# State-space mixer: decay, convolution and gate work moved from GpSimd to VectorE and ScalarE

## Chip, cores and metric

The kernel runs on one core of a Trainium2 chip. The metric is device time in microseconds of one execution; the numbers of record are the median over several executions. Engines are named as in the profile: PE is TensorE, DVE is VectorE, ACT is ScalarE, POOL is GpSimd, SP is the engine whose queue issues most DMAs.

## The reference, cut to what matters

The program is a stack of twelve units (attention, state space, feed-forward, mixture of experts). The change touches one of them, a bidirectional state-space mixer over 256 positions, 32 heads of 64, 8 groups of B and C with state size 128:

```python
def ssd_mixer(h, w_in, conv_w, conv_b, dt_bias, a_log, d_skip, norm_g, w_out):
    z, xbc, dt_raw = split(h @ w_in)
    xbc = silu(centred_depthwise_conv(xbc, conv_w, conv_b))      # 5 taps
    xs, b_f, c_f, b_b, c_b = split(xbc)
    dt = softplus(dt_raw + dt_bias)
    a = -exp(a_log)
    y_fwd = ssd_scan(xs, dt[:, :, 0], a[0], b_f, c_f)
    y_bwd = flip(ssd_scan(flip(xs), flip(dt[:, :, 1]), a[1], flip(b_b), flip(c_b)))
    y = y_fwd + y_bwd + xs * d_skip
    return rmsnorm_2(y * silu(z), norm_g) @ w_out

def ssd_scan(x, dt, a, b_mat, c_mat):                            # chunks of 128
    cum = cumsum(dt * a)
    seg = cum[t] - cum[s]
    scores = (C[t] . B[s]) * exp(where(s <= t, seg, -inf)) * dt[s]
    y = scores @ x          # and, across the chunk border, the same with the decay over it
```

## The kernel before, in words

All weights are f32 in HBM and reach SBUF as tiles of 1 MB (`wraw`), by DMAs on SP's queue in program order; three raw tiles are held. Every tile is split on chip into a rounded part and a rest: ACT writes `whi` (L211), DVE subtracts it and writes `wlo` (L212), in two halves of 128x1024 each; three split tiles are held. A projection of 256 output columns is 48 matmuls (L269): for each of 8 k-blocks and 2 column blocks three products, of `whi` and `wlo` with the two parts `hh` and `hl` of the activations. Results stand in three PSUM banks `pj`; four banks `acc` serve the scan.

The mixer (`ssd`, L1920) runs over 8 groups g. For each group it projects four tiles, in the order x, f (B and C forward), b (B and C backward), z:

- `conv` (L1929) evacuates x, f or b from PSUM with the norm's row factor (`cz`, L1931, DVE), starts the convolution on ACT (L1936) and adds four more taps to each of two halves: by `stt` (L287, DVE, in place in `cvx`, `cvf`, `cvb`), but for the second half of x by a product `cvt` (L1942) and a sum (L1943) on POOL. ACT applies silu (L1947).
- `ssd_decay` (L1896) makes the decays of a group for both directions r: SP loads the group's rows of the cumulative sums, broadcast to 128 partitions, into `crow` (two DMAs of 512 KB, one buffer). POOL subtracts the per-partition part (L1911), adds the causal mask, 0 or -1e30 (L1912), for the two diagonal blocks, and adds the offset of the block between the chunks (L1915). ACT takes exp in place (L1917). The tile `E` is 128x4x3x128 (4 heads, 3 blocks), in three buffers.
- `scan` (L1956) transposes x on PE, copies it to `xd` (ACT, L1966), multiplies B with C on PE into a PSUM bank (6 matmuls of 128 columns) and multiplies `E` by that bank on DVE (L1975, 128x1536, ahead in priority by 100).
- `scan_out` (L1978) multiplies `E` with `xd` on PE (16 matmuls a group, `acc<-E,xd`), adds the skip term on DVE (two `stt`), multiplies by the gate `sz` on POOL (L1990), splits the result into `yh` (ACT, L1994) and `yl` (DVE), and sums its squares (ACT L410, POOL L419 and L420).

In the program text the loop over g projects x, f, then runs `scan(g-1)`, projects b and z, then runs `scan_out(g-1)` and `ssd_decay(g)`. After the loop come `scan(7)`, `scan_out(7)` and the output projection: 8 tiles of 48 matmuls (`acc<-yh,whi` and the like, 384 in all). A scheduler orders each engine's instructions at build time, from program order and the priorities in the text; at run time each engine, and SP's queue, takes its list strictly in order and waits on semaphores.

Of the kernel before, what the change touches and what calls it, by code (L numbers as in the profile page):

```python
# [27 lines left out]
NEG = -1e30  # L28

# [217 lines left out]
class Kernel:  # L247
# [1587 lines left out]
    def ssd_consts(self, pool):  # L1835
        nc = self.nc
        S = self.S = {}
        S["mask"] = [pool.tile([128, 128], F32, name=f"smask{i}") for i in range(2)]
        for m, op in zip(S["mask"], (OP.is_lt, OP.is_gt)):
            nc.vector.tensor_scalar(m, self.jp, 0.0, NEG, op0=op, op1=OP.mult)  # L1840
        go = S["go"] = pool.tile([64, T], F32, name="sgo")
        nc.gpsimd.memset(go, 1.0)
        nc.gpsimd.memset(go.rearrange("p (c i) -> p c i", i=128)[:, :, 0:1], 0.0)
        na = S["na"] = pool.tile([64, 32], F32, name="sna")[:, 0:1]
        nc.scalar.activation(na, self.v["a_log"][:64, :], AF.Exp)
        nc.vector.tensor_scalar(na, na, -1.0, None, op0=OP.mult)
        S["cz"] = {}
        for n, k in (("x", 2), ("f", 1), ("b", 1)):
            for i in range(k):
                z = S["cz"][n, i] = pool.tile([128, 2, T + 4], F32, name=f"cz{n}{i}")  # L1850
                nc.gpsimd.memset(z[:, :, 0:2], 0.0)
                nc.gpsimd.memset(z[:, :, T + 2:T + 4], 0.0)

    def ssd_dt(self, pool, b, r):
# [31 lines left out]
        for o, c, l in ((0, 0, 127), (32, 1, 128)):  # L1886
            rs, cs = slice(o, o + 32), slice(c * 128, (c + 1) * 128)
            self.stt(off[rs], dt[rs, cs], cum[rs, l:l + 1], cum[rs, cs], OP.add, OP.subtract)
        v.tensor_sub(p, cum, dt)
        b = self.bank("ms")  # L1890
        for i, src in enumerate((p[:, 0:128], p[:, 128:256], off)):
# [4 lines left out]
    def ssd_decay(self, pool, g):  # L1896


        nc, S = self.nc, self.S
        cr = pool.tile([128, 2, 4, T], F32, name="crow", bufs=1)  # L1900
        src = S["dram"].rearrange("(r h) t -> r h t", r=2)[:, 4 * g:4 * g + 4, :]
        for r in range(2):
            nc.sync.dma_start(cr[:, r], src[r][None].to_broadcast([128, 4, T]))
        out = []
        for r in range(2):
            E = pool.tile([128, 4, 3, 128], F32, name="E", bufs=3)
            hs = slice(4 * g, 4 * g + 4)
            for c in range(2):
                d = E[:, :, 2 * c, :]
                cc = S["tok"][:, c, r, hs][:, :, None].to_broadcast([128, 4, 128])  # L1910
                nc.gpsimd.tensor_sub(d, cr[:, r, :, c * 128:(c + 1) * 128], cc)  # L1911
                nc.gpsimd.tensor_add(d, d, S["mask"][r][:, None, :].to_broadcast([128, 4, 128]))  # L1912
            oc = S["tok"][:, 2, r, hs][:, :, None].to_broadcast([128, 4, 128])
            t = slice(128, 256) if r == 0 else slice(0, 128)
            nc.gpsimd.tensor_add(E[:, :, 1, :], cr[:, r, :, t], oc)  # L1915
            out.append(E)
            nc.scalar.activation(E, E, AF.Exp)  # L1917
        return out

    def ssd(self, pool, tail):  # L1920
# [8 lines left out]
        def conv(n, g, b):  # L1929
# [7 lines left out]
            for k in range(1, 5):  # L1937
                for j in range(2):
                    w = cw[:, 48 * k + tl[j]:48 * k + tl[j] + 1]
                    if n == "x" and j:  # L1940
                        t = pool.tile([128, T], F32, name="cvt", bufs=1)
                        nc.gpsimd.tensor_mul(t, z[:, j, k:k + T], w.to_broadcast([128, T]))  # L1942
                        nc.gpsimd.tensor_add(c[:, j], c[:, j], t)  # L1943
                    else:
                        self.stt(c[:, j, :], z[:, j, k:k + T], w, c[:, j, :], OP.mult, OP.add)
# [10 lines left out]
        def scan(g, tag="acc"):  # L1956
# [10 lines left out]
            for r, bc in enumerate((fb, bb)):  # L1967
# [4 lines left out]
                cb = b[:, None, 0:384].to_broadcast([128, 4, 384])  # L1972
                e = E[r].rearrange("p h i t -> p h (i t)")
                with self.tc.high_priority(offset=100):
                    v.tensor_mul(e, e, cb)  # L1975
            D_["s", g] = E, xs, xd, sz

        def scan_out(g, tag="acc"):  # L1978
# [11 lines left out]
            nc.gpsimd.tensor_mul(sz, sz, xs)  # L1990
# [19 lines left out]
        for g in range(8):  # L2010
            for n in "xfb":
                if (n, g) != ("x", 0):
                    self.proj([("ssd", n, g)], lambda i, b: conv(n, g, b))
                if n == "f" and g:
                    scan(g - 1)
            self.proj([("ssd", "z", g)], lambda i, b: gate(g, b))
            if g:
                scan_out(g - 1)
            D_["E", g] = self.ssd_decay(pool, g)
# [496 lines left out]
```

## Time and profile before

| what | value |
|---|---|
| median of 3 runs | 2814.09 us (2808.49 to 2814.82) |
| the profiled execution | 2806.44 us |
| its span in the trace | 2804.6 us |
| the mixer's part of the span | from about 1677 us to 2024 us |
| DVE, PE, ACT, POOL busy, whole span | 78%, 93%, 56%, 20% |

The span is the time between the first and the last instruction in the trace; the profiled execution's own time is 1.8 us longer. Busy shares are unions over an engine's instructions. "Idle before" in a row is the time in which the engine stood still just ahead of those instructions, with what ended it. A row's busy time divided by its count is what one instruction takes of its engine when they follow each other; the mean ns is longer, since the start of one overlaps the end of the one before.

### The profile page before, as it was taken

The numbers are of one execution on the slowest core, as the hardware profiler recorded it, in microseconds if no ns is written. First come the engines' busy times: TensorE is split into PE (matmuls) and PEld (weight loads), VectorE is DVE, ScalarE is ACT, GpSimd is POOL, SyncE is SP. The second block draws the span as 40 slices with busy tenths as digits, with TensorE's granted clock in tenths as the row PEclk, the third lists the DMA queues.
The fourth block names the chain that finished last, engine by engine and source line by source line (L and its number), as shares of the span: only waits on it lengthen the run. The fifth ranks groups of instructions, "written<-read, shape, count | busy, mean of one in ns | idle before, by whom it ended". The sixth has DMA issues, their size and how long they took to land. (4 is left out here: it accounts for less than half of the span.)

```text
span 2804.6 us, 50551 instructions
## 1 busy us (share of the span) xinstructions
PE 2622.2 (93%) x20739; PEld 2446.0 (87%) x20739; DVE 2178.5 (78%) x3100; ACT 1582.7 (56%) x2222; POOL 564.0 (20%) x490
## 2 busy tenths in 40 slices
PE   8999968989999999999998998887899999989999
PEld 6789967789999999999778997777799999979998
DVE  6989986869998999988876568999665675665666
ACT  5343336657777777777663445766444454465444
POOL 2413982310000000000000005776110010240000
PEclk9999988999999999999998999999999999999999
DMA  7476764256999999999763554434445555552553
GB/s 276 167 270 248 279 210 150 91 214 258 349 338 355 339 353 365 342 325 372 250 213 140 197 178 152 151 139 147 151 166 196 186 175 193 195 188 72 182 194 121
DMA packets 109203, 623.07 MB, mean 222 GB/s; under 512 B 10049, under 2 KB 10065, under 8 KB 56353
## 3 DMA queue, kind: packets, MB, share of 16 engines
q1 hardware_dynamic: 107664, 612.05, 61.2%
q0 software_dynamic: 1296, 7.68, 0.7%
q8 instruction: 165, 2.70, 0.4%
q14 instruction: 78, 0.63, 0.1%
HBM read 616.49 MB, written 3.21 MB: 221 GB/s over the span
## 5 line engine op out<-in xcount | busy, mean ns | idle before, releaser
L212 DVE TENSOR_TENSOR wlo<-wraw,whi 128x1024 fp32r<-128x1024 f32 (+1 forms) x1046 | 1284.3, 1265 | 250.1 <-ACT whi L211 247.3
L211 ACT ACTIVATE whi<-wraw 128x1024 fp32r<-128x1024 f32 (+1 forms) x1046 | 1046.5, 1050 | 668.6 <-issue 353.8
L269 PE MATMUL pj<-hh,whi 128*128 128x256 f32 (+1 forms) x2672 | 757.8, 284 | 54.0 <-DVE czb L1931 38.5
L269 PE MATMUL pj<-hh,wlo 128*128 128x256 f32 (+1 forms) x2672 | 754.3, 282 | 4.1 <-DVE wlo L212 4.0
L269 PE MATMUL pj<-hl,whi 128*128 128x256 f32 (+1 forms) x2672 | 754.2, 282 | 1.2 <-DVE hl L287 1.2
L269 PEld LDWEIGHTS pj<-hh,whi 128*128 128x128 f32 (+1 forms) x2672 | 514.9, 193 | 58.9 <-issue 29.3
L269 PEld LDWEIGHTS pj<-hh,wlo 128*128 128x128 f32 (+1 forms) x2672 | 514.4, 193 | 7.9 <-DVE wlo L212 6.8
L269 PEld LDWEIGHTS pj<-hl,whi 128*128 128x128 f32 (+1 forms) x2672 | 514.8, 193 | 3.0 <-DVE hl L287 2.3
L269 PE MATMUL pj<-whi,hg 128*128 128x256 f32 x2112 | 382.2, 279 | 0.0
L269 PEld LDWEIGHTS pj<-whi,hg 128*128 128x128 f32 x2112 | 325.6, 188 | 11.2 <-issue 8.7
L269 PE MATMUL pj<-wlo,hg 128*128 128x256 f32 x1056 | 294.0, 278 | 0.0
L269 PE MATMUL acc<-mh,whi 128*128 128x256 f32 x880 | 245.5, 279 | 13.9 <-ACT whi L211 13.9
L269 PE MATMUL acc<-mh,wlo 128*128 128x256 f32 x880 | 245.8, 279 | 7.0 <-DVE wlo L212 7.0
L269 PE MATMUL acc<-ml,whi 128*128 128x256 f32 x880 | 245.7, 279 | 1.6 <-DVE ml L284 1.6
L269 PEld LDWEIGHTS pj<-wlo,hg 128*128 128x128 f32 x1056 | 198.6, 188 | 3.7 <-issue 2.1
L269 PEld LDWEIGHTS acc<-mh,whi 128*128 128x128 f32 x880 | 167.2, 190 | 14.1 <-ACT whi L211 14.1
L441 POOL TENSOR_TENSOR rc<-var,mhalf 128x2 f32<-128x2 f32 x2 | 1.4, 705 | 878.4 <-DVE var L1803 877.1
L417 POOL TENSOR_TENSOR ss<-sq 128x256 f32<-128x256 f32 x11 | 11.9, 1083 | 825.1 <-ACT sq L410 592.2
L269 PEld LDWEIGHTS acc<-mh,wlo 128*128 128x128 f32 x880 | 167.1, 190 | 8.1 <-DVE wlo L212 8.1
L269 PEld LDWEIGHTS acc<-ml,whi 128*128 128x128 f32 x880 | 167.1, 190 | 2.2 <-DVE ml L284 2.2
L269 PE MATMUL acc<-whi,mml 128*128 128x512 f32 x352 | 139.1, 399 | 0.7 <-DVE mml L284 0.7
L269 PE MATMUL acc<-wlo,mmh 128*128 128x512 f32 x352 | 139.6, 397 | 0.0
(721 smaller groups left out, 4424.6 us busy)
## 6 DMA issues: line engine op xcount, KB each, us to landing
wraw<-in_o_exp_down_dram SPq DMA_DIRECT2D x88, 1024.0 KB, 5.8
wraw<-in_ffn_w_gu_dram SPq DMA_DIRECT2D x88, 1024.0 KB, 5.0
wraw<-in_o_exp_gate_dram SPq DMA_DIRECT2D x87, 1024.0 KB, 5.9
wraw<-in_o_exp_up_dram SPq DMA_DIRECT2D x87, 1024.0 KB, 6.0
wraw<-in_ffn_w_down_dram SPq DMA_DIRECT2D x44, 1024.0 KB, 5.1
wraw<-in_ssd_cols_dram SPq DMA_DIRECT2D x32, 1024.0 KB, 4.9
wraw<-in_e_mod_ffn_w_t_dram SPq DMA_DIRECT2D x12, 1024.0 KB, 5.0
wraw<-in_o_mod_mix_w_t_dram SPq DMA_DIRECT2D x12, 1024.0 KB, 5.0
```

Source lines behind the costliest of these rows:

```text
L211: nc.scalar.activation(hi[:, cs], t[:, cs], AF.Copy)
L212: nc.vector.tensor_sub(lo[:, cs], t[:, cs], f32(hi[:, cs]))
L269: self.nc.tensor.matmul(out, lhsT, rhs, start=start, stop=stop, skip_group_check=True)
L417: nc.gpsimd.tensor_add(ss[0], sq[:, 0, :], sq[:, 1, :])
L441: nc.gpsimd.tensor_tensor(r, v, self.mhalf.to_broadcast([128, n]), op=OP.pow)
```

## The change

The masks become factors 0 and 1. Both blocks' per-partition parts and the block between the chunks now have one sign, so that one subtraction serves all three blocks. SP loads the broadcast rows straight into `E` (four DMAs a group: two of 4x256 and two of 4x128 elements per partition, in pieces of 1024 and 512 bytes; 1.5 MB in place of 1 MB), now with four buffers for `E` and none for `crow`. DVE subtracts (one 128x1536 instruction a direction) and limits the diagonal blocks to 88.722 (one `min` over 1024 elements). ACT takes exp as before. The mask is multiplied onto the product of B and C on its way out of PSUM (`scb`: DVE two blocks, ACT copies the third), and the product with `E` reads `scb` from SBUF. The second half of x's convolution and the gate product go to DVE. `ssd_decay(g)` is called right after x's projection of group g. POOL keeps only the sums of squares.

```diff
--- before.py
+++ after.py
@@ -26,6 +26,8 @@
 MID = 3
 EPS = 1e-6
 NEG = -1e30
+
+LOGMAX = 88.722
 
 SPLIT_ORDER = {"s": -30, "f1_0": -100, "e": -200, "f2_0": 50}
 
@@ -1836,8 +1838,8 @@
         nc = self.nc
         S = self.S = {}
         S["mask"] = [pool.tile([128, 128], F32, name=f"smask{i}") for i in range(2)]
-        for m, op in zip(S["mask"], (OP.is_lt, OP.is_gt)):
-            nc.vector.tensor_scalar(m, self.jp, 0.0, NEG, op0=op, op1=OP.mult)
+        for m, op in zip(S["mask"], (OP.is_ge, OP.is_le)):
+            nc.vector.tensor_scalar(m, self.jp, 0.0, None, op0=op)
         go = S["go"] = pool.tile([64, T], F32, name="sgo")
         nc.gpsimd.memset(go, 1.0)
         nc.gpsimd.memset(go.rearrange("p (c i) -> p c i", i=128)[:, :, 0:1], 0.0)
@@ -1885,10 +1887,10 @@
         off = s2[:, 0:128]
         for o, c, l in ((0, 0, 127), (32, 1, 128)):
             rs, cs = slice(o, o + 32), slice(c * 128, (c + 1) * 128)
-            self.stt(off[rs], dt[rs, cs], cum[rs, l:l + 1], cum[rs, cs], OP.add, OP.subtract)
+            self.stt(off[rs], cum[rs, cs], cum[rs, l:l + 1], dt[rs, cs], OP.subtract, OP.subtract)
         v.tensor_sub(p, cum, dt)
         b = self.bank("ms")
-        for i, src in enumerate((p[:, 0:128], p[:, 128:256], off)):
+        for i, src in enumerate((p[:, 0:128], off, p[:, 128:256])):
             self.tr(b[:, 64 * i:64 * (i + 1)], src)
         tok = S["tok"] = pool.tile([128, 3, 2, 32], F32, name="stok")
         v.tensor_copy(tok, b[:, :192].rearrange("p (i r h) -> p i r h", i=3, r=2))
@@ -1896,24 +1898,19 @@
     def ssd_decay(self, pool, g):
 
 
+
         nc, S = self.nc, self.S
-        cr = pool.tile([128, 2, 4, T], F32, name="crow", bufs=1)
         src = S["dram"].rearrange("(r h) t -> r h t", r=2)[:, 4 * g:4 * g + 4, :]
-        for r in range(2):
-            nc.sync.dma_start(cr[:, r], src[r][None].to_broadcast([128, 4, T]))
         out = []
         for r in range(2):
-            E = pool.tile([128, 4, 3, 128], F32, name="E", bufs=3)
-            hs = slice(4 * g, 4 * g + 4)
-            for c in range(2):
-                d = E[:, :, 2 * c, :]
-                cc = S["tok"][:, c, r, hs][:, :, None].to_broadcast([128, 4, 128])
-                nc.gpsimd.tensor_sub(d, cr[:, r, :, c * 128:(c + 1) * 128], cc)
-                nc.gpsimd.tensor_add(d, d, S["mask"][r][:, None, :].to_broadcast([128, 4, 128]))
-            oc = S["tok"][:, 2, r, hs][:, :, None].to_broadcast([128, 4, 128])
-            t = slice(128, 256) if r == 0 else slice(0, 128)
-            nc.gpsimd.tensor_add(E[:, :, 1, :], cr[:, r, :, t], oc)
+            E = pool.tile([128, 4, 3, 128], F32, name="E", bufs=4)
+            for i, n, t in ((0, 2, 0), (2, 1, 128)) if r == 0 else ((0, 1, 0), (1, 2, 0)):
+                nc.sync.dma_start(E[:, :, i:i + n, :].rearrange("p h i t -> p h (i t)"), src[r][None, :, t:t + n * 128].to_broadcast([128, 4, n * 128]))
             out.append(E)
+        for r, E in enumerate(out):
+            cc = S["tok"][:, :, r, 4 * g:4 * g + 4].rearrange("p i h -> p h i")
+            nc.vector.tensor_sub(E, E, cc[:, :, :, None].to_broadcast([128, 4, 3, 128]))
+            nc.vector.tensor_scalar(E[:, :, 0::2, :], E[:, :, 0::2, :], LOGMAX, None, op0=OP.min)
             nc.scalar.activation(E, E, AF.Exp)
         return out
 
@@ -1937,12 +1934,7 @@
             for k in range(1, 5):
                 for j in range(2):
                     w = cw[:, 48 * k + tl[j]:48 * k + tl[j] + 1]
-                    if n == "x" and j:
-                        t = pool.tile([128, T], F32, name="cvt", bufs=1)
-                        nc.gpsimd.tensor_mul(t, z[:, j, k:k + T], w.to_broadcast([128, T]))
-                        nc.gpsimd.tensor_add(c[:, j], c[:, j], t)
-                    else:
-                        self.stt(c[:, j, :], z[:, j, k:k + T], w, c[:, j, :], OP.mult, OP.add)
+                    self.stt(c[:, j, :], z[:, j, k:k + T], w, c[:, j, :], OP.mult, OP.add)
             with self.tc.high_priority(offset=-100) if n == "x" else nullcontext():
                 nc.scalar.activation(c, c, AF.Silu)
             D_[n, g] = c
@@ -1969,10 +1961,13 @@
                 c0, c1 = slice(0, 128), slice(128, 256)
                 for i, (s, t) in enumerate(((c0, c0), (c0, c1) if r == 0 else (c1, c0), (c1, c1))):
                     self.mm(b[:, i * 128:(i + 1) * 128], bc[:, 0, s], bc[:, 1, t], i == 0, i == 2)
-                cb = b[:, None, 0:384].to_broadcast([128, 4, 384])
+                cb = pool.tile([128, 3, 128], F32, name="scb", bufs=2)
+                b = b[:, 0:384].rearrange("p (i t) -> p i t", i=3)
                 e = E[r].rearrange("p h i t -> p h (i t)")
                 with self.tc.high_priority(offset=100):
-                    v.tensor_mul(e, e, cb)
+                    v.tensor_mul(cb[:, 0::2], b[:, 0::2], S["mask"][r][:, None, :].to_broadcast([128, 2, 128]))
+                    nc.scalar.activation(cb[:, 1], b[:, 1], AF.Copy)
+                    v.tensor_mul(e, e, cb.rearrange("p i t -> p (i t)")[:, None, :].to_broadcast([128, 4, 384]))
             D_["s", g] = E, xs, xd, sz
 
         def scan_out(g, tag="acc"):
@@ -1987,7 +1982,7 @@
             for j in range(2):
                 d = 2 * g + j
                 self.stt(xs[:, j, :], xs[:, j, :], self.v["ssd_d"][:, d:d + 1], yb[:, j * T:(j + 1) * T], OP.mult, OP.add)
-            nc.gpsimd.tensor_mul(sz, sz, xs)
+            v.tensor_mul(sz, sz, xs)
             gn = self.v["ssd_norm"]
             for j in range(2):
                 d = 2 * g + j
@@ -2013,10 +2008,11 @@
                     self.proj([("ssd", n, g)], lambda i, b: conv(n, g, b))
                 if n == "f" and g:
                     scan(g - 1)
+                if n == "x":
+                    D_["E", g] = self.ssd_decay(pool, g)
             self.proj([("ssd", "z", g)], lambda i, b: gate(g, b))
             if g:
                 scan_out(g - 1)
-            D_["E", g] = self.ssd_decay(pool, g)
         row = {}
 
         def t2(p, acc):

```

The change also moves the order on three engines. DVE, one group in the middle of the stage, before (`cz` is the evacuation of a projection, `wlo` the split, `E<-E,acc` the product with B times C):

```order
L1931 TENSOR_TENSOR czx_21747<-pj,rstd 128x2x256
L287 SCALAR_TENSOR_TENSOR yl<-sz,vecs,yh 128x256 x2
L212 TENSOR_TENSOR wlo<-wraw,whi 128x1024 x2
L287 SCALAR_TENSOR_TENSOR cvx<-czx_21747,vecs,cvx 128x256 x3
L1931 TENSOR_TENSOR czf_21750<-pj,rstd 128x2x256
L287 SCALAR_TENSOR_TENSOR cvx<-czx_21747,vecs,cvx 128x256
L1975 TENSOR_TENSOR E<-E,acc 128x1536 x2
L212 TENSOR_TENSOR wlo<-wraw,whi 128x1024 x2
L287 SCALAR_TENSOR_TENSOR cvf<-czf_21750,vecs,cvf 128x256 x8
L212 TENSOR_TENSOR wlo<-wraw,whi 128x1024 x2
L1931 TENSOR_TENSOR czb_21753<-pj,rstd 128x2x256
L1952 TENSOR_TENSOR sz<-pj,rstd 128x512
```

and in the changed kernel, from the products of one group to the evacuation of b in the next (`E<-E,scb` is the product, `E<-E,stok` the new subtraction, the row of form 128x4x2x128 the `min`):

```order
L1970 TENSOR_TENSOR E<-E,scb 128x1536 x2
L1928 TENSOR_TENSOR czx_21747<-pj,rstd 128x2x256
L1912 TENSOR_TENSOR E<-E,stok 128x1536
L289 SCALAR_TENSOR_TENSOR cvx<-czx_21747,vecs,cvx 128x256 x8
L1913 TENSOR_SCALAR E<-E 128x4x2x128
L1912 TENSOR_TENSOR E<-E,stok 128x1536
L214 TENSOR_TENSOR wlo<-wraw,whi 128x1024
L1913 TENSOR_SCALAR E<-E 128x4x2x128
L214 TENSOR_TENSOR wlo<-wraw,whi 128x1024
L1928 TENSOR_TENSOR czf_21750<-pj,rstd 128x2x256
L214 TENSOR_TENSOR wlo<-wraw,whi 128x1024 x2
L289 SCALAR_TENSOR_TENSOR cvf<-czf_21750,vecs,cvf 128x256 x8
L1928 TENSOR_TENSOR czb_21753<-pj,rstd 128x2x256
```

The subtractions, the eight in place of four additions of x and the two `min` now stand between x's evacuation and f's; the products with `E` stand ahead of x's evacuation.

SP's queue, before, in the middle of the stage (`wraw` are the weight tiles, `crow` the broadcast rows):

```order
L1903 DMA crow<-cumd 128x1024 x2
L181 DMA wraw<-in_ssd_cols_dram 128x2048 x4
L1903 DMA crow<-cumd 128x1024 x2
L181 DMA wraw<-in_ssd_cols_dram 128x2048 x4
L1903 DMA crow<-cumd 128x1024 x2
L181 DMA wraw<-in_ssd_cols_dram 128x2048 x3
```

and now:

```order
L183 DMA wraw<-in_ssd_cols_dram 128x2048 x4
L1908 DMA E<-cumd 128x4x256
L1908 DMA E<-cumd 128x4x128 x2
L1908 DMA E<-cumd 128x4x256
L183 DMA wraw<-in_ssd_cols_dram 128x2048 x4
L1908 DMA E<-cumd 128x4x256
L1908 DMA E<-cumd 128x4x128 x2
L1908 DMA E<-cumd 128x4x256
```

Four loads stand where two stood, and counted from the start of the stage they lie directly ahead of the weight tile z of their own group.

PE at the end of the stage, before (`acc<-yh,whi` and the like are output projection, `pj<-E,xd` the last group's scan):

```order
L269 MATMUL pj<-cvb 128x128 x3
L269 MATMUL pj<-E,xd 64x256 x4
L269 MATMUL pj<-E,xd 64x128 x4
L269 MATMUL acc<-yh,whi 128x256
L269 MATMUL acc<-yl,whi 128x256
L269 MATMUL acc<-yh,wlo 128x256
L269 MATMUL acc<-yh,whi 128x256
L269 MATMUL acc<-yl,whi 128x256
L269 MATMUL pj<-E,xd 64x256 x4
L269 MATMUL pj<-E,xd 64x128 x4
L269 MATMUL acc<-yh,wlo 128x256
```

and now:

```order
L271 MATMUL acc<-yh,wlo 128x256
L271 MATMUL acc<-yh,whi 128x256
L271 MATMUL acc<-yl,whi 128x256
L271 MATMUL acc<-yh,wlo 128x256
L271 MATMUL acc<-yh,whi 128x256
L271 MATMUL pj<-E,xd 64x256 x4
L271 MATMUL pj<-E,xd 64x128 x4
L271 MATMUL acc<-yl,whi 128x256
L271 MATMUL acc<-yh,wlo 128x256
```

Before, 45 of the output projection's 384 matmuls stand ahead of the last block of `pj<-E,xd`; now 121 do.

## Rows read from the trace of the kernel before

**Rows 1.** The page: head, part 1 (busy), and from part 5 ACT's half of the split.
```profile
span 2804.6 us, 50551 instructions
...
PE 2622.2 (93%) x20739; PEld 2446.0 (87%) x20739; DVE 2178.5 (78%) x3100; ACT 1582.7 (56%) x2222; POOL 564.0 (20%) x490
...
L211 ACT ACTIVATE whi<-wraw 128x1024 fp32r<-128x1024 f32 (+1 forms) x1046 | 1046.5, 1050 | 668.6 <-issue 353.8
```
**Rows 2.** Windows view, the stage: length, PE, PEld, DVE, ACT, POOL busy, clock, DMA.
```profile
1694.00:1986.00 292.00, 229.02 (x1853) 217.99 (x1854) 274.08 (x321) 183.59 (x222) 192.37 (x163) 0.89 0.41 143
```
**Rows 3.** Waits view, 1680 to 2030 us: waited in total, times, longest.
```profile
PE pj L269 <- DVE czb L1931: 48.8, 7, 10.3
```
**Rows 4.** Lines view by form, DVE, 1694 to 1986 us.
```profile
L212 DVE TENSOR_TENSOR wlo<-wraw,whi 128x1024 fp32r<-128x1024 f32 x62 | 93.9, 1544 | 0.0
L287 DVE SCALAR_TENSOR_TENSOR cvf<-czf,vecs,cvf 128x256 f32<-128x256 f32 x64 | 60.9, 1002 | 0.0
L287 DVE SCALAR_TENSOR_TENSOR cvx<-czx,vecs,cvx 128x256 f32<-128x256 f32 x32 | 26.8, 837 | 0.2
L287 DVE SCALAR_TENSOR_TENSOR cvb<-czb,vecs,cvb 128x256 f32<-128x256 f32 x64 | 26.4, 478 | 0.2
L1975 DVE TENSOR_TENSOR E<-E,acc 128x1536 f32<-128x1536 f32 x14 | 23.9, 1744 | 6.2 <-ACT E L1917 6.2
L287 DVE SCALAR_TENSOR_TENSOR yl<-sz,vecs,yh 128x256 fp32r<-128x256 f32 x12 | 11.4, 986 | 10.0 <-ACT yh L1994 10.0
...
L1952 DVE TENSOR_TENSOR sz<-pj,rstd 128x512 f32<-128x512 f32 x8 | 5.4, 679 | 0.0
...
L1869 DVE TENSOR_TENSOR dtq<-dts 64x256 f32<-64x256 f32 x1 | 0.4, 407 | 0.0
...
L1894 DVE COPY stok<-ms 128x192 f32<-128x192 f32 x1 | 0.4, 358 | 0.1
...
L1870 DVE TENSOR_SCALAR dtp<-dtq 64x256 f32<-64x256 f32 x1 | 0.3, 274 | 0.0
```
**Rows 5.** Lines view by form, POOL, 1694 to 1986 us.
```profile
L420 POOL TENSOR_TENSOR ssb<-ssb,sq 128x256 f32<-128x256 f32 x5 | 5.9, 1173 | 0.2
L419 POOL TENSOR_TENSOR sq<-sq 128x256 f32<-128x256 f32 x5 | 4.4, 885 | 0.6 <-ACT sq L410 0.6
```
**Rows 6.** Timeline, DVE, one group: start, length of the merged row, what.
```profile
1890.83 7.65 DVE L287 SCALAR_TENSOR_TENSOR cvf<-czf,vecs,cvf 128x256 f32<-128x256 f32 x8
...
1902.02 3.35 DVE L287 SCALAR_TENSOR_TENSOR cvb<-czb,vecs,cvb 128x256 f32<-128x256 f32 x8
1905.30 2.36 DVE L212 TENSOR_TENSOR wlo<-wraw,whi 128x1024 fp32r<-128x1024 f32 x2
```
**Rows 7.** Timeline, POOL, the same group; in brackets the idle time before.
```profile
1889.78 3.21 POOL L1911 TENSOR_TENSOR E<-crow,stok 128x512 f32<-128x512 f32 x2
...
1895.80 1.22 POOL L1915 TENSOR_TENSOR E<-crow,stok 128x512 f32<-128x512 f32 x1
1908.44 1.04 POOL L1911 TENSOR_TENSOR E<-crow,stok 128x512 f32<-128x512 f32 x1 [11.43 <-DVE cvx L287]
```
**Rows 8.** DMA view, 1738 to 1748 us, two `crow` loads alone: packets, MB, share.
```profile
q1 hardware_dynamic: 288, 1.05, 32.3%
...
crow<-cumd SPq DMA_DIRECT2D x2, 512.0 KB, 4.3
```
**Rows 9.** DMA view, 2797.5 to 2799.5 us, one store in pieces of 2 KB.
```profile
q1 hardware_dynamic: 144, 0.26, 34.8%
```
**Rows 10.** The page, part 6: issues, KB each, us to landing.
```profile
wraw<-in_ssd_cols_dram SPq DMA_DIRECT2D x32, 1024.0 KB, 4.9
```
**Rows 11.** Chain of waits by time, 1660 to 2040 us: start, us, what.
```profile
1809.43 3.33 DVE E L1975 x2
...
1957.92 3.33 DVE E L1975 x2
...
1987.99 34.47 PE acc L269 x291
```

## The prediction

> **What bounds the kernel now.** I read the page first. Over the whole span PE is busy 93% of the time and POOL 20% [rows 1], but such a share mixes twelve units; the change touches one, so the stage counts. Second, the windows view of the state-space stage, from the first evacuation to the last product with E, 292 us long: DVE is busy 274.1 us of it, POOL 192.4, PE 229.0, ACT 183.6 [rows 2]. DVE has 17.9 us to spare, PE 63. Third, the waits: PE's longest total, 48.8 us in 7 waits, ends with DVE's evacuation of b [rows 3]. The stage is DVE's, and PE waits for it.
>
> Fourth, DVE by instruction [rows 4]. The same form, a `stt` over 128x256, takes 60.9/64 = 0.95 us in f's convolution and 26.4/64 = 0.41 us in b's. The two timelines of one group say why: the eight of f fill 7.65 us from 1890.83 [rows 6], and POOL runs its work on E without a gap from 1889.78 to 1897.0 [rows 7]; the eight of b fill 3.35 us from 1902.02 [rows 6], inside a pause of POOL of 11.43 us that ends at 1908.44 [rows 7]. So DVE's instructions with two SBUF inputs stretch while POOL works. Those that read PSUM do not: L1975 keeps 1744 ns on average over 14 [rows 4] with POOL busy two thirds of the stage.
>
> Last, the chain: the five pairs of products from 1809.43 to 1957.92 give 148.5/4 = 37.1 us a group, and behind the stage PE alone ends things, 291 matmuls in 34.47 us, 0.118 us each [rows 11].
>
> **What DVE gets back.** Per instruction I divide busy time by count. Undisturbed values are 0.41 us for the `stt` and 2.36/2 = 1.18 us for `wlo`, which stood in POOL's pause too [rows 6]. Then `wlo` gives 62 x (93.9/62 - 1.18) = 20.7 us, f's taps 64 x (0.95 - 0.41) = 34.5, x's 32 x (26.8/32 - 0.41) = 13.6, `yl` 12 x (0.95 - 0.41) = 6.5 [rows 4]. Sum: 75 us.
>
> **What DVE takes over.**
> - The other half of x's taps: 32 x 0.41 = 13.2 us.
> - The subtractions: 16 over 128x1536. The product of that size takes 23.9/14 = 1.71 us [rows 4]; 16 x 1.71 = 27.3.
> - The `min`: 16 over 1024 elements. No row has it. The upper end is `wlo`, 1024 elements with two inputs, 1.18. The lower end is from two rows of 64x256: one input 274 ns, two inputs 407 [rows 4]; the difference of 133 ns is half of the 267 ns that 256 elements would take at the rate of 0.96 elements per ns which such rows show (the step from 256 to 512 elements, 407 to 679 ns, is 272). So an instruction with one input runs at twice the rate: 1.18 - 0.53 = 0.65 us. I take that, as the nearest kind: 10.4 us; the upper end is 18.9.
> - The masked evacuation `scb`: 16 over 256 elements out of PSUM, between the rows for 192 (358 ns) and 512 (679 ns) [rows 4]; about 0.42 us: 6.7.
> - The gate product: 8 over 512 elements at 0.68: 5.4.
> - The products with E stay; they read SBUF in place of PSUM, priced equal.
>
> Sum: 63.0 us, with the upper end 71.5. DVE's work goes from 274.1 to 274.1 - 75 + 63 = 262 us.
>
> **What POOL keeps.** The sums of squares, two instructions a group, 1.2 and 0.9 us, 10.3 us in the rows [rows 5] and about 12 with the first group's. Here a rule stands against the change. The rows show that L1975 with its input in PSUM was never stretched [rows 4], while the new product, the new subtraction and the gate product all read two SBUF inputs: the change makes more of DVE's time touchable than before. The Trainium skill (SBUF — State Buffer, section "SBUF: two separate sides") says that a VectorE instruction with two SBUF inputs, or in a two-port mode, and a GpSimd instruction that reads SBUF exclude one another for a whole instruction: whichever starts first holds the shared port pair. By that rule up to all of POOL's remaining time would be charged to DVE. From the rows alone the charge lies between nothing (POOL's instructions fall beside evacuations out of PSUM) and 12 us; I take the middle, 6. DVE: 268 us.
>
> **What of DVE's idle time goes.** 10.0 us stood before `yl`, behind ACT's `yh`, which waited for POOL's gate product; with the product on DVE, other work (`scb`, a `wlo` or a product) is queued between gate product and `yl`. 6.2 us stood before the products, waiting for exp [rows 4], whose input came late from POOL. Both kinds shrink; for new waits on the loads of E and on the copy of `scb` I leave 8 us of the 17.9. Stage: 268 + 8 = 276 us against 292, a gain of 16.
>
> **The end of the stage.** By the order, 121 of the output projection's matmuls now stand ahead of the last scan block, 45 before. Those 76 run while PE would wait, and are missing behind the stage: 76 x 0.118 = 9.0 us [rows 11]. The lower end is nothing, if DVE's splits of those tiles come too late.
>
> ACT gains two small copies a group and loses one of two table changes for exp a group by its order; at 184 of 292 us it covers either. The DMAs change from 1.05 MB to 1.57 MB a group; what covers them is DVE's time, and the price if the cover fails is the first rival.
>
> **The sum.** 16 + 9 = 25 us off. Against the profiled execution, 2806.4 (span 2804.6 and 1.8 around it), that is 2781; that execution was 7.6 us below the median of the runs shown, and the forecast for a median is 2814.1 - 25 = **2789 us**. From no change a measurement here can tell about 0.3%, 8.4 us. The forecast's own ends: with no charge from POOL, 3 us of idle time and somewhat cheaper work, 38 us off, 2776; with the `min` at the upper end (8.5), the full charge (6) and half the end effect (4.5), 6 us off, 2808.
>
> **Rival 1, slower: the loads of E hold up the weights.** In SP's order the four loads of a group stand ahead of that group's tile z, and they wait until PE has finished the scan block of two groups earlier, which frees the buffer. Tiles z and the next x wait behind them. The ring is: the loads (x us of transfer and 1.1 us fixed, the 4.3 us to landing less 3.2 of transfer [rows 8]); the two tiles behind, 1 MB each at the same 3.2; ACT's rounding of the second, 2 x 1.05 [rows 1], which stands ahead of the convolution's start on ACT; eight taps of x, 3.3; a subtraction, two `min` and two `wlo`, 5.4; the projection of z, 48 x 0.118 = 5.7; then the scan block. Sum: x + 24. The pieces are new: 2048 a group, of 512 and 1024 bytes. By bytes the two `crow` loads, 1.05 MB in 32.3% of 10 us [rows 8], give x = 4.8. A piece of 4 KB (256 of them, 128 partitions twice) cost 32.3% of 10 us x 16 / 256 = 0.20 us of a DMA engine there, one of 2 KB 34.8% of 2 us x 16 / 128 = 0.087 [rows 9]: smaller pieces were cheaper by at least their bytes, which is why I take x = 5 to 6 and a ring of 30 us, hidden under DVE's 35 (37.1 x 276/292). If a small piece cost what one of 2 KB costs, x = 11 and the ring is 35, still level; it decides from x = 13, where it reaches today's 37.1, 0.10 us a piece. At 0.145, midway between both rows, x = 18.5, the ring 42.5: 7 x 5.4 = 38 us lost, 9 won at the end, **2843 us**. For it: no row has pieces between 0.4 and 2 KB, let alone so many in a DMA. Against it: the fall from 4 to 2 KB. A tile alone lands in 4.9 us [rows 10], so nothing else fills the DMAs.
>
> **Rival 2: the whole of POOL's rest is charged to DVE**, by the rule above: 6 us more, **2795 us**. For it: f's eight taps needed 7.65 us with POOL at work and 3.35 without. Against it: the rest is short and much of DVE's work reads PSUM.
>
> **Rival 3, no change: the new work costs its upper ends.** The `min` at 1.18, the full charge, and no end effect, since PE takes its tiles no earlier: 25 - 8.5 - 6 - 9 = 2 us off, **2812 us**.
>
> **Rival 4, slower: DVE's instructions were not stretched by POOL**, and only part of the 75 us comes back. With half, the stage is 16 - 37 = 21 us longer, **2826 us** after the end effect. Against it speak the two timelines.
>
> That the change would not do what it says I rule out: the order has no row of POOL on E, x or the gate.
>
> **How the numbers follow.** Forecast 0.58, rival 2 0.12, rival 3 0.13, rival 1 0.12, rival 4 0.05. Faster: 0.58 + 0.12 = 0.70; same 0.13; slower 0.17. The range takes the forecast's ends, rivals 2 and 3 and a run's scatter, 2774 to 2816; it leaves the two slower rivals out.
>
> **What would show it.** In the profile of the changed kernel f's taps should fill about 3.4 us a group and `wlo` take 1.2; the `min` 0.65; DVE should be busy for over 95% of a stage some 16 us shorter; the run of PE alone behind the stage should hold about 215 matmuls and last 25 us. Waits of the subtraction for a DMA, or SP's waits ahead of E growing into PE's waits for `wlo`, would show rival 1; a `min` above 1 us, rival 3. An f convolution still above 6 us a group would prove the whole reasoning wrong.

## The result, and the profile after

The changed kernel takes 2777.4 us (median of 4 runs, 2772.2 to 2781.4) against 2811.3 for the kernel before beside it (4 runs): ratio 0.9879, 95% interval 0.9854 to 0.9905, so 34 us faster, between 27 and 41. Forecast were 25 us.

The profiled executions stand 34.3 us apart (2806.44 and 2772.16), their spans 34.2. To see where, I cut each span at two marks on DVE's timeline: the mixer begins with the first evacuation of x (1693.93 us before, 1690.53 after) and ends with the first addition of the output projection to the residual (2029.50 and 1994.92). Between the marks lie 335.6 us before and 304.4 after: **31.2 us are the mixer's**, the other 3.0 lie in code that the change does not touch. That code took 2466 to 2487 us in the profiles of this study but for two of the experiments, so below I compare mixers, not medians. One execution of each kernel was profiled, and no run shows how far a mixer scatters by itself; e6 and e12, whose extra work should cost DVE nothing, lie within 1.2 us of the changed kernel, so I read little into differences of some 2 us. The part up to the end of the last product with E is the stage: 292.2 us before, 267.8 after, 24.4 less. The part behind it went from 43.3 to 36.6 us, 6.8 less.

The windows view of the changed kernel, stage and the stretch behind it (length; PE, PEld, DVE, ACT, POOL busy; granted clock; DMA share; GB/s):

```profile
1690.53:1958.34 267.81, 234.39 (x1920) 220.55 (x1920) 263.84 (x409) 169.89 (x224) 11.13 (x13) 0.96 0.51 174
1958.34:1989.15 30.81, 30.81 (x259) 30.23 (x258) 17.92 (x20) 14.62 (x17) 1.39 (x2) 0.97 0.56 199
```

Beside [rows 2], POOL's 192 us are down to 11, and DVE stands still for 4.0 us only. It is more than ever the stage's engine: 98.5% busy.

DVE's rows in that stage (lines view by form: count, busy, mean ns, idle before):

```profile
L214 DVE TENSOR_TENSOR wlo<-wraw,whi 128x1024 fp32r<-128x1024 f32 x62 | 75.8, 1238 | 0.0
L1970 DVE TENSOR_TENSOR E<-E,scb 128x1536 f32<-128x1536 f32 x16 | 28.8, 1815 | 1.1 <-ACT E L1914 0.9 <-ACT scb L1969 0.2
L1912 DVE TENSOR_TENSOR E<-E,stok 128x1536 f32<-128x1536 f32 x16 | 27.9, 1746 | 0.0
L289 DVE SCALAR_TENSOR_TENSOR cvf<-czf,vecs,cvf 128x256 f32<-128x256 f32 x64 | 26.4, 475 | 0.0
L289 DVE SCALAR_TENSOR_TENSOR cvx<-czx,vecs,cvx 128x256 f32<-128x256 f32 x64 | 26.3, 473 | 0.0
L289 DVE SCALAR_TENSOR_TENSOR cvb<-czb,vecs,cvb 128x256 f32<-128x256 f32 x64 | 26.1, 476 | 0.0
L1913 DVE TENSOR_SCALAR E<-E 128x1024 f32<-128x1024 f32 x16 | 10.9, 684 | 0.0
L289 DVE SCALAR_TENSOR_TENSOR yl<-sz,vecs,yh 128x256 fp32r<-128x256 f32 x13 | 8.7, 702 | 0.1
...
L1968 DVE TENSOR_TENSOR scb<-acc,smask 128x256 f32<-128x256 f32 x14 | 5.6, 417 | 1.0 <-PE acc L271 1.0
...
L1985 DVE TENSOR_TENSOR sz<-sz,cvx 128x512 f32<-128x512 f32 x7 | 4.8, 682 | 0.0
```

Against [rows 4]: f's taps fell from 60.9 us to 26.4 and are now equal to b's; `wlo` fell from 93.9 to 75.8; the 10.0 us of idle time before `yl` and the 6.2 before the products are gone. New are the subtraction, the `min`, `scb` and the gate product.

PE's waits for DVE's evacuations, 48.8 us in [rows 3], in the waits view from 1640 to 2030 us:

```profile
PE pj L271 <- DVE czf L1928: 16.6, 6, 2.9
...
PE pj L271 <- DVE czb L1928: 3.8, 3, 3.2
```

In the chain of waits one direction's subtraction comes back seven times from 1732.12 to 1928.87:

```profile
1732.12 1.67 DVE E L1912
...
1928.87 1.66 DVE E L1912
```

That is (1928.87 - 1732.12)/6 = 32.8 us a group, where it took 37.1 before [rows 11].

### The profile page after: what moved, and what is told of

Read it like the earlier page. It is cut to its first block, busy times and chain, and to the rows that moved or that the text cites. A ratio compares the mean times of both kernels' runs of the same rounds, so it can differ in the third digit from the quotient of the medians.

```text
span 2770.4 us, 50520 instructions
## 1 busy us (share of the span) xinstructions
PE 2620.2 (95%) x20739; PEld 2441.5 (88%) x20739; DVE 2168.6 (78%) x3188; ACT 1566.1 (57%) x2224; POOL 379.7 (14%) x338
## 5 line engine op out<-in xcount | busy, mean ns | idle before, releaser
L214 DVE TENSOR_TENSOR wlo<-wraw,whi 128x1024 fp32r<-128x1024 f32 (+1 forms) x1046 | 1264.7, 1245 | 242.8 <-ACT whi L213 239.7
L271 PE MATMUL acc<-whi,mmh 128*128 128x512 f32 x352 | 137.3, 406 | 0.0
L271 PE MATMUL pj<-whi,hgx 128*128 128x256 f32 x704 | 126.2, 278 | 0.0
```

The costliest lines, as they stand in the source:

```text
L214: nc.vector.tensor_sub(lo[:, cs], t[:, cs], f32(hi[:, cs]))
L271: self.nc.tensor.matmul(out, lhsT, rhs, start=start, stop=stop, skip_group_check=True)
```

## The experiments

All twelve are read by the same marks (us; "idle" is DVE's in the stage; the ratio is to the kernel before run beside it, with its interval):

| kernel | mixer | stage | DVE busy | idle | POOL busy | median, ratio |
|---|---|---|---|---|---|---|
| before | 335.6 | 292.2 | 274.3 | 17.9 | 192.4 | 2811.3 |
| changed | 304.4 | 267.8 | 263.8 | 4.0 | 11.1 | 2777.4, 0.9879 (0.9854 to 0.9905) |
| e1 changed, x on POOL | 326.0 | 290.4 | 276.6 | 13.7 | 97.0 | 2801.0, 0.9969 (0.9945 to 0.9994) |
| e2 changed, gate on POOL | 303.4 | 268.3 | 260.5 | 7.8 | 29.9 | 2780.6, 0.9887 (0.9849 to 0.9926) |
| e3 before, x on DVE | 334.5 | 292.4 | 265.8 | 26.6 | 144.3 | 2812.0, 0.9999 (0.9981 to 1.0017) |
| e4 before, gate on DVE | 333.3 | 290.0 | 281.9 | 8.0 | 182.4 | 2812.2, 1.0008 (0.9987 to 1.0028) |
| e5 changed, POOL reads twice | 343.6 | 308.6 | 303.5 | 5.1 | 93.3 | 2842.1, 1.0107 (1.0070 to 1.0145) |
| e6 changed, POOL only writes | 303.2 | 268.1 | 262.8 | 5.4 | 40.8 | 2781.6, 0.9888 (0.9851 to 0.9924) |
| e7 changed, decays late | 302.2 | 273.2 | 264.1 | 9.1 | 20.7 | 2774.2, 0.9865 (0.9821 to 0.9908) |
| e8 subtraction in exp | 285.0 | 248.3 | 241.9 | 6.3 | 12.0 | 2765.9, 0.9842 (0.9799 to 0.9884) |
| e9 changed, x and gate on POOL | 327.1 | 290.7 | 271.8 | 18.8 | 112.0 | 2801.9, 0.9972 (0.9948 to 0.9996) |
| e10 as e8, grouped | 310.4 | 271.4 | 244.8 | 26.6 | 13.3 | 2785.9, 0.9913 (0.9887 to 0.9939) |
| e11 changed, POOL reads once | 355.4 | 320.1 | 271.8 | 48.3 | 119.1 | 2846.9, 1.0121 (1.0077 to 1.0164) |
| e12 changed, loads twice | 303.8 | 268.2 | 261.7 | 6.5 | 15.7 | 2787.6, 0.9912 (0.9885 to 0.9939) |

### Does POOL hold DVE up, and which work of POOL's? (e5, e6, e11)

Three kernels add ten POOL instructions a group behind the sums of squares; only the instruction differs (the scratch tile `dm` is made once, ahead of the loop):

```diff
             self.sq_add(g, sz, ssy, last=7)
+            for _ in range(10):
+                nc.gpsimd.tensor_sub(S["dm"], S["dm"], S["dm"])                   # e5
+                nc.gpsimd.memset(S["dm"], 0.0)                                    # e6
+                nc.gpsimd.tensor_scalar(S["dm"], S["dm"], 0.0, None, op0=OP.mult) # e11
```

> The changed kernel with ten extra POOL instructions a group behind the sums of squares: a subtraction of a scratch tile from itself, 128x512, the form and size of POOL's former work on E, whose result nothing uses. Theory: 70 of them fall in the stage, 1.04 us each when alone, 73 us; DVE pays for 54% to 85% of that, 39 to 62 us: 2816 to 2839 us, with f's taps, b's taps or wlo stretched wherever these run. Rival (what stretched DVE before was not POOL): no change, 2777 us, DVE's rows as they were.

> The changed kernel with ten extra POOL memsets a group of a scratch tile of 128x512 in the same place: POOL writes SBUF and reads nothing. If only POOL's reading of SBUF holds DVE up: at most 3 us slower, 2777 to 2780 us, with no row of DVE's two-input instructions longer. If any POOL instruction does: 70 memsets at 0.3 to 0.5 us (estimate: half of the two-input instruction's 1.04 or less), 54% to 85% of it charged, 11 to 30 us, 2788 to 2807 us.

> The changed kernel with ten extra POOL instructions a group that read SBUF once: a scratch tile of 128x512 times a constant, in the place of the earlier subtractions and memsets. If any reading of SBUF by POOL holds DVE's two-input instructions up: 60 of them in the stage, 0.5 to 1.04 us each alone, 65% of it charged (39.7 us of DVE time for 60 subtractions of 1.04), 20 to 40 us slower than the changed kernel, 2797 to 2817 us. If only POOL's second input does: at most 3 us, 2777 to 2780 us, with DVE's rows as they were.

One thing I had not foreseen: nothing ties the extra instructions to their group, so they ran in one unbroken block from the mixer's start. The same place in the program then shows all three cases: b's eight taps of the first group, each time with POOL inside that block. DVE's timeline in e5, e6 and e11:

```profile
1765.87 10.00 DVE L289 SCALAR_TENSOR_TENSOR cvb<-czb,vecs,cvb 128x256 f32<-128x256 f32 x8
```
```profile
1724.26 3.25 DVE L289 SCALAR_TENSOR_TENSOR cvb<-czb,vecs,cvb 128x256 f32<-128x256 f32 x8
```
```profile
1750.45 4.37 DVE L289 SCALAR_TENSOR_TENSOR cvb<-czb,vecs,cvb 128x256 f32<-128x256 f32 x8
```

And POOL's timeline of the block (e5: one instruction that DVE did not hold up, then two pieces; e6; e11):

```profile
1684.35 1.03 POOL L1995 TENSOR_TENSOR dm<-dm 128x512 f32<-128x512 f32 x1
...
1707.51 64.11 POOL L1995 TENSOR_TENSOR dm<-dm 128x512 f32<-128x512 f32 x45
1771.57 0.58 POOL L1885 DMA_DIRECT2D cumd<-dtx  x1
1772.17 32.09 POOL L1995 TENSOR_TENSOR dm<-dm 128x512 f32<-128x512 f32 x20
```
```profile
1720.57 11.63 POOL L1995 MEMSET dm<- 128x512 f32 x20
```
```profile
1713.75 77.41 POOL L1995 TENSOR_SCALAR dm<-dm 128x512 f32<-128x512 f32 x45
```

Against POOL's subtractions the eight taps need 10.00 us in place of 3.25, against memsets 3.25. POOL suffers too: 32.09/20 = 1.60 us for an instruction that takes 1.03 when nothing holds it up. Inside the 10.00 us the two engines take turns. One turn of each in e5's timeline:

```profile
1769.34 1.10 POOL L1995 TENSOR_TENSOR dm<-dm 128x512 f32<-128x512 f32 x1
1769.47 1.25 DVE L289 SCALAR_TENSOR_TENSOR cvb<-czb,vecs,cvb 128x256 f32<-128x256 f32 x1
```

The turns before and after start at 1768.16 and 1770.52 us on POOL and hold one tap each: 1.18 us a turn, where the two take 1.03 and 0.41 undisturbed. So the times add up but for 0.26 us, by which a turn overlaps the next. Over the stage 60 subtractions cost DVE 303.5 - 263.8 = 39.7 us, 0.66 us each, the lower end of what was expected. The rival without contention is out, and a memset costs nothing: e6's mixer is that of the changed kernel, and its median, 1.6 us above what was expected, lies within the scatter of its runs. POOL's instruction with one input is another case. It takes 1.49 us while DVE stands still (77.41/45 = 1.72 over the block), and it cost the eight taps 4.37 - 3.25 = 1.1 us. Single instructions of DVE in e11's timeline, of one form, come in two lengths:

```profile
1732.99 0.82 DVE L289 SCALAR_TENSOR_TENSOR dtp<-dtp,dtq 64x256 f32<-64x256 f32 x1
1734.34 0.41 DVE L289 SCALAR_TENSOR_TENSOR dtp<-dtp,dtq 64x256 f32<-64x256 f32 x1
```

One that meets the start of POOL's instruction waits 0.41 us; three of the eight taps did. So it holds DVE for about a quarter of its length, and my two expectations for e11 were both off.

The medians of e5 and e11 hold more than that. The block also delayed POOL's part of the norm in front of the mixer (the mixer starts at 1716.91 and 1721.40 us) and, in e11, the store of the cumulative sums, which is issued from POOL's queue: DVE stood still for 43.49 us for the first loads of E, which wait for that store. A queue that runs in order makes a spare engine's filler work a delay for whatever is queued behind it.

### What each part is worth (e1, e2, e3, e4, e9)

```diff
 e1, e9: the second half of x's taps as cvt and a sum on POOL again
 e2, e9
-            v.tensor_mul(sz, sz, xs)
+            nc.gpsimd.tensor_mul(sz, sz, xs)
 e3: kernel before, all of x's taps by stt on DVE
 e4: kernel before, v.tensor_mul(sz, sz, xs)
```

> The changed kernel with one part undone: the second half of x's convolution back on POOL (64 instructions of 128x256). Theory: while POOL's instructions with SBUF inputs run, DVE's instructions with two SBUF inputs wait, so POOL's work is paid for by DVE. DVE gives 13.2 us of taps back; POOL takes on 35 to 51 us (64 at 0.55 to 0.8), of which 54% (75 us of stretch for some 139 us of POOL work in the kernel before) to 85% (the share of DVE's time now in such instructions) is charged: 19 to 43 us. About 6 to 30 us slower than the changed kernel, 2783 to 2807 us, with wlo above 1.3 us or f's taps above 0.5 us each. Rival (POOL's help is free, DVE's time is its own instructions alone): 13 us faster, 2764 us.

> The changed kernel with one part undone: the gate product back on POOL. Theory: DVE loses 5.4 us of work; POOL's eight products of 1.0 to 1.57 us are charged for 5 to 10 us, and the wait in front of yl for ACT's yh, 10 us in the kernel before and 0.1 in the changed one, comes back in part: 0 to 15 us slower than the changed kernel, 2777 to 2792 us. Rival (the 10 us of waiting went away through the new order of DVE's instructions, not through the product's move): 5 us faster, 2772 us, with DVE's idle time before yl below 2 us.

> The kernel before with one part of the change: all of x's taps on DVE, 32 more. Theory: the taps cost DVE 13 us undisturbed, up to 25 where POOL's work on E overlaps them; POOL's 64 instructions (57 us in the rows, 35 to 51 undisturbed) stop stretching the rest, worth 54% of that, 19 to 28 us. Between 15 us faster and 6 us slower than the kernel before, 2796 to 2817 us, the middle 2805. Rival (no stretching by POOL): 13 us slower or more, 2824 us.

> The kernel before with one part of the change: the gate product on DVE. Theory: 5.4 us more work on DVE, 10.0 us of waiting before yl gone, and 4 us less stretching: 4 to 9 us faster than the kernel before, 2802 to 2807 us. Rival (the wait goes elsewhere, to the products with E that wait for exp): 0 to 5 us slower, 2811 to 2816 us.

> The changed kernel with two parts undone, so that only the decays and the mask have moved: the second half of x's convolution and the gate product are on POOL. Theory (POOL's reading work and DVE's two-input work exclude each other, so a part pays as long as the rest of POOL's work still fits beside DVE's reads of PSUM): as with x alone on POOL, within 6 us of that run's mixer (320 us of 298.6 in the changed kernel), 2794 to 2807 us; the decays alone are worth 4 to 12 us and x's move, worth 1 us in the kernel before, the other 20. Rival (each part has one price, 1 us for x and 2 for the gate as measured on the kernel before): 3 us slower than the changed kernel, 2780 us.

e9 puts the steps in a row: the decays alone take 335.6 to 327.1, 8.5 us; the gate product on top 1.1; x on top of that 21.6, to 304.4. On the kernel before, x alone (e3) is worth 1.1 us and the gate alone (e4) 2.3. The parts have no price of their own, and the rival of e9 is out. Of the 8.5 us only 1.6 lie in the stage (292.2 to 290.7), the rest behind it; 22.6 of the stage's 24.4 us come with the last step, x, which is worth nothing in e3. The small steps, 1.1 and 2.3, can't be told from none, and the medians of e3 and e4 show none. (The 320 and 298.6 us in e9's expectation were read up to the norm. In e9 the norm stands ahead of most of the output projection, so only the mark at the residual compares like with like.)

Why does x pay nothing in e3, whose median of 2812.0 lies at the far end of the expected range? DVE did get work back there: 274.3 to 265.8 us, although 13.2 us of taps came on. But its idle time grew by as much, 17.9 to 26.6. DVE's wait before b's taps, which is 0.2 us in [rows 4], and the chain of waits of e3 around the first half of it:

```profile
L287 DVE SCALAR_TENSOR_TENSOR cvb<-czb,vecs,cvb 128x256 f32<-128x256 f32 x64 | 33.6, 593 | 10.3 <-ACT cvb L1936 10.3
```

```profile
1783.91 0.89 PE acc L269 x12
1784.87 4.35 POOL E L1911 x2
1789.22 3.48 POOL E L1912 x2
1792.70 1.01 POOL E L1915
1793.77 1.34 issue
1795.12 0.60 ACT cvb L1936
1796.23 2.08 DVE cvb L287 x5
1798.38 2.40 POOL E L1911 x2
1800.78 3.42 POOL E L1912 x2
1804.20 1.99 POOL E L1915
1806.21 1.48 ACT E L1917
1807.71 1.28 ACT L1942
1809.00 0.64 ACT cvb L1942
1809.68 1.65 PE acc L269 x6
1811.33 13.35 PE pj L269 x96
```

PE's scan block frees a buffer of E, POOL makes the decays in it, ACT's list holds exp ahead of b's silu, and PE's products of B and C wait for that. One round of this ring takes 41 us, from the end of PE's projection at 1783.3 to the next at 1824.7, where a group took 37.1 before. The 10.3 us are 5.4 and 4.9, in two groups; from 1848 us on the chain runs mostly over DVE again. So a ring through POOL lay close to DVE's load and came up in part of the stage when DVE was relieved. That it alone ate x's gain is not shown; that it needs the decays' move to go away is argued from the chain.

In e1, with the decays on DVE, x on POOL costs 22.6 us of stage. DVE's rows that show it:

```profile
L1975 DVE TENSOR_TENSOR E<-E,scb 128x1536 f32<-128x1536 f32 x16 | 33.4, 2088 | 0.0
...
L289 DVE SCALAR_TENSOR_TENSOR cvx<-czx,vecs,cvx 128x256 f32<-128x256 f32 x32 | 29.7, 928 | 0.8 <-ACT cvx L1933 0.8
L289 DVE SCALAR_TENSOR_TENSOR cvb<-czb,vecs,cvb 128x256 f32<-128x256 f32 x64 | 26.8, 479 | 9.0 <-ACT cvb L1933 8.9
...
L1913 DVE TENSOR_SCALAR E<-E 128x1024 f32<-128x1024 f32 x16 | 16.8, 1047 | 0.0
```

Half the taps cost 29.7 us where all of them cost 26.3; the products rise by 4.6 us and the `min` from 10.9 to 16.8. 12.8 us more of DVE with 13.2 us less to do, and 9.7 us more of idle time. The signs that e1's expectation named did not come: `wlo` takes 74.2/62 = 1.20 us and f's taps 26.5/64 = 0.41. POOL's work on x fell beside x's own taps, the subtractions, the `min` and the products instead.

The gate product is a wash on either kernel. In e4 the wait before `yl` went from 10.0 to 0.7 us, as expected, but DVE's busy time rose by 7.6 where 1.4 had been reckoned (5.4 of work less 4 of stretching); the median, 2812.2, lies in the rival's range, though not for the rival's reason, since the wait before the products did not grow (4.7 us for 6.2). In e2 the wait did not come back (0.0 before `yl`): the rival was right that the new order hides it, while the 5 us did not come: 5.4 us of waiting for PE stand before `scb`.

### Place and loads (e7, e12)

```diff
 e7: D_["E", g] = self.ssd_decay(pool, g) back at the end of the loop's body
 e12, in ssd_decay
-                nc.sync.dma_start(E[...], src[...])
+                for _ in range(2):
+                    nc.sync.dma_start(E[...], src[...])
```

> The changed kernel with one part undone: the decays of a group are called at the end of the group's pass through the loop, where the kernel before called them, and not after x's projection. Theory: DVE's sum of work sets the stage, and it is the same: within 6 us of the changed kernel, 2771 to 2783 us. Rival (it was the earlier place that took DVE's 14 us of idle time away and put more of the output projection ahead of the last scan block): 10 to 20 us slower, 2787 to 2797 us, with idle time before the products with E and fewer output-projection matmuls ahead of the last block.

> The changed kernel with each load of E issued twice to the same place; the second waits for the first to land and holds SP's queue meanwhile. Theory (DVE sets the stage and the loads are hidden): 0 to 3 us slower, 2777 to 2780 us. The prediction's first rival (a ring of x + 24 us through the loads, the weights behind them and the scan): x grows from 5 or 6 to at least 10 to 12 us, the ring to 34 to 36 us against a group's 32.8: 8 to 22 us slower, 2785 to 2799 us, with SP's waits ahead of E and PE's waits for wlo or DVE's waits for E's loads.

e7's mixer is 2.2 us shorter, not longer: the earlier place did not make the gain. Its stage is 5.4 us longer and the part behind it 7.6 shorter, 29.0 against 36.6, so the two are one account: what PE does not do in the stage it does behind it.

e12's median lies in the rival's range, its profile does not: the mixer is 0.6 us shorter, though the loads took their packets twice (DMA share in the stage 0.66 against 0.51), and the subtraction's row has 0.1 us of idle time before it:

```profile
L1913 DVE TENSOR_TENSOR E<-E,stok 128x1536 f32<-128x1536 f32 x16 | 27.8, 1750 | 0.1
```

What e12's span has more lies outside the mixer, where no edit reaches (2483 us against 2466), and its interval overlaps the changed kernel's. I count the ring through the loads as refuted for the mixer. Its x was not measured by itself; in the changed kernel the loads of E land 3.6 to 10.5 us after their issue, 6.0 in the median (tile view), beside weight tiles in the same queue.

### Relieving DVE further (e8, e10)

```diff
 e8, in ssd_decay (tok is now negated, tokm is 88.722 minus tok; e10: both min, then all exp, each at priority 400)
-            nc.vector.tensor_sub(E, E, cc...)
-            nc.vector.tensor_scalar(E[:, :, 0::2, :], E[:, :, 0::2, :], LOGMAX, None, op0=OP.min)
-            nc.scalar.activation(E, E, AF.Exp)
+            nc.vector.tensor_tensor(E[:, :, 0::2, :], E[:, :, 0::2, :], ccm..., op=OP.min)
+            for h in range(4):
+                for i in range(3):
+                    nc.scalar.activation(E[:, h, i, :], E[:, h, i, :], AF.Exp, bias=S["tok"][...])
```

> The changed kernel with DVE relieved: the subtraction goes into exp on ACT as its per-partition bias, twelve pieces of 128x128 in place of one instruction of 128x1536, and the limit becomes a minimum of two tensors over the diagonal blocks (1024 elements). DVE loses 27.9 + 10.9 us and gains 16 x 1.18 = 18.9: 20 us less, 244 us. ACT gains 16 x (12 x 0.25 - 1.48) = 24 us, 194 us. Theory (DVE sets the stage): 15 to 20 us faster than the changed kernel, 2757 to 2762 us, with PE, 234 us busy, soon the next bound. Rival (ACT's exp in twelve pieces comes too late for the products with E): less than 8 us of gain, 2769 us or more, with DVE waiting for ACT before the products.

> The version with the subtraction as exp's bias on ACT, with the minimum and the exp pieces of both directions put together by priority: 14 fewer table changes on ACT by its order, 14 x 1.28 = 18 us less of ACT's 228 us, the same work on DVE (242 us). Theory (DVE still sets the stage): within 5 us of the version before it, 2760 to 2770 us. Rival (ACT, busy for 92% of that stage, holds it by now): 8 to 15 us faster than it, 2751 to 2758 us.

The stage of e8 and that of e10, in the windows view:

```profile
1699.75:1948.03 248.28, 224.68 (x1902) 212.60 (x1903) 241.94 (x390) 228.47 (x419) 12.01 (x12) 0.97 0.55 183
```
```profile
1688.32:1959.73 271.41, 234.21 (x1891) 221.89 (x1892) 244.80 (x391) 212.10 (x405) 13.27 (x12) 0.92 0.50 169
```

e8 takes 21.9 us off DVE and 19.5 off the stage: nearly one for one, the best test that DVE sets it. Its mixer is 19.4 us shorter than the changed kernel's, as expected. By median it is 11.5 us faster, 2765.9, between the two expected ranges; the two kernels were not run beside each other, and their intervals against the kernel before overlap. ACT paid 59 us, not 24: the pieces took 59.6/192 = 0.31 us each in place of 0.25, and the scheduler mixed them with silu, so that ACT changes tables 40 times in place of 18, at 1.28 us. e10 removed 14 of these changes and lost 25 us: in DVE's list, fixed at build time, the minimum and the products now stand where they must wait (before `scb` 7.9 us for PE, before the minimum 6.3 for the loads, before the products 5.3 for ACT). Both of its expectations were wrong. Neither DVE (244.8 us busy) nor ACT (212.1) fills that stage of 271.4 us; I put it down to the order, which was not varied by itself.

## Why the prediction was right, and where it was short

- **The bound.** Right, and shown by e8: DVE's work goes into the stage nearly one for one. Left out was the ring through POOL's decays that e3 shows. It did the forecast no harm, since the change takes the decays off POOL.
- **What DVE gets back.** f's taps 34.5 us, as forecast, x's 13.6, as forecast; `wlo` 18.1 for 20.7; the 12 `yl` in the forecast's window 3.7 for 6.5. e5 shows the mechanism, and the trace of the kernel before agrees instruction by instruction: 43 of f's 64 taps overlap one of POOL's instructions and take 1.26 us on average, the other 21 take 0.47.
- **What DVE takes over.** x's taps 13.2 for 13.2, subtractions 27.9 for 27.3, `min` 10.9 for 10.4, `scb` 6.4 for 6.7, gate product 0.68 us each as forecast. The `min`, which no row showed, was well bounded by the two small rows.
- **POOL's charge.** What `wlo` and `yl` fell short (2.6 + 2.8), and the 1.4 us by which the products exceed 16 x 1.71, make 6.8; I took 6. Not all of the 6.8 is POOL's: a `wlo` that stands alone fills more than the 1.18 us taken from a pair. What the instructions that overlap one of POOL's take beyond the others of their kind is 1.5 us for `wlo`, 2.9 for `yl` and 1.1 for the products, 5.5 in all. The 6 was the middle of a range and not a reading, so its nearness is luck. The Trainium skill (SBUF — State Buffer, section "SBUF: two separate sides") lets a two-input VectorE instruction contend only with a GpSimd instruction that reads SBUF; e5 and e6 agree (10.00 us for eight taps, and 3.25). It has the lock held for the whole instruction; e5's turns of 1.18 us come near that, e11's 0.41 us of 1.49 does not, for an instruction with one input, and the measurement decides.
- **DVE's sum, mis-sized by 4.3 us.** By rows the forecast was 274.1 - 75 + 63 + 6 = 268, 6.1 less. All of DVE's rows add up to 287.4 us before and 281.2 after: 6.2 less, so the sum by rows was right. But in the union they are 274.3 and 263.8: neighbours of different rows lie over each other by 13.1 us before and 17.4 after, with 87 more instructions. I had taken each new instruction at its row's full length.
- **DVE's idle time, mis-sized by 4.0 us.** Of 17.9 us I left 8; 4.0 remain. The waits I made room for, on E's loads and on the copy of `scb`, are 0.0 and 0.2 us. Together with the 4.3: stage 24.4 in place of 16.
- **The end of the stage.** 6.8 us for 9.0. Behind the last product, up to the norm, PE still runs 259 matmuls where it ran 324: 65 fewer, not 76, and not down to the 215 named as a sign. 65 x 0.118 = 7.7. The rest is, by an estimate, the granted clock, which was 1.00 in that stretch before and is 0.97 now: 0.03 x 30.81 = 0.9 us.
- **The rivals.** The ring through the loads did not show, nor did doubled loads bring it (e12). The whole of POOL's rest was not charged. The `min` at 1.18 us did not come. DVE's stretching is POOL's (e5). That E has four buffers in place of three was not tested by itself.

So 31.2 us in the mixer for 25: right in mechanism and sign, short by 8.4 us in the stage and long by 2.2 behind it. The two errors in the stage have one direction, and the sum over parts that the forecast made is not how the gain comes about (e3, e9): it held because all parts were moved together.

## What to carry to other kernels

Price work on POOL that reads two SBUF inputs as work on DVE when DVE is busy with two-input instructions from SBUF: the two engines take turns (1.18 us for a pair that takes 0.41 and 1.03 alone), and moving the work to DVE can even shorten DVE's own time. Judge a change of several parts as a whole: relieving the busiest engine can be worth nothing (e3) while other parts of the change are missing. And cut a profile at two marks around the edited part before comparing: here the untouched rest scatters by more than several of the effects.

## What the runs showed that I had not expected

- A POOL memset beside DVE's two-input instructions is free (3.25 us for eight taps, the undisturbed value), and a POOL instruction with one input holds DVE for 0.41 us of its 1.49.
- DVE's instruction with one SBUF input, at twice the rate, is stretched as well: the `min` takes 1.05 us in e1 and 0.68 in the changed kernel.
- PE's granted clock in the stage rose from 0.89 to 0.96 as PE's idle time fell from 63 to 33 us, and was 0.87 in e11, where PE idled for 80 us. The windows view of the changed kernel shows one such fall, behind a wait of PE of 2.93 us for b's silu (PE's timeline, then the windows):

```profile
1953.96 1.65 PE L271 MATMUL pj<-cvb 128*128 128x128 f32 x6 [2.93 <-ACT cvb L1939]
...
1953.90:1958.30 4.40, 4.34 (x22) 3.03 (x23) 3.38 (x6) 2.31 (x6) 0.09 (x1) 0.50 0.00 0
1958.30:1960.00 1.70, 1.70 (x10) 1.70 (x9) 1.70 (x3) 0.00 (x0) 1.43 (x2) 0.50 0.00 0
1960.00:1965.00 5.00, 5.00 (x46) 4.42 (x46) 3.29 (x6) 3.19 (x4) 0.00 (x0) 0.99 0.00 0
```

For 6 us PE works at 0.50, the lower level of 1.2 GHz, and then at 2.4 GHz again. The forecast had no term for it. What it is worth in a stage that DVE sets, no run separates.
